# Earlier gates, copies and weight releases in the sublayer heads, a reordered mixer and moved buffers, in a two-layer trunk on one core

## The chip, the cores and the metric

The kernel runs on one core of one Trainium2 chip. The metric is the device time of one execution in microseconds, from a median of runs. The core's engines work beside each other, each through its own instructions in order: TensorE (PE, with its weight loads as PEld) multiplies matrices, VectorE (DVE) and ScalarE (ACT) work elementwise and move results out of the matmul banks, GpSimd (POOL) takes a few elementwise operations, and SyncE (SP) issues the DMA transfers.

## What is computed

The reference is a trunk of two layers on 512 tokens of width 1024 in float32. Each layer has a mixer and a feed-forward network (FFN), and each of the four sublayers is wrapped in the same way:

```python
def sandwich(x, mod, g_pre, g_post, fn):
    shift, scale, gate = mod
    h = rms_norm(x, g_pre) * (1.0 + scale[:, None]) + shift[:, None]
    return x + gate[:, None] * rms_norm(fn(h), g_post)

def swiglu(h, w_in, w_out):
    a, b = jnp.split(h @ w_in, 2, axis=-1)
    return (jax.nn.silu(a) * b) @ w_out

def modulation(c, w, b):
    return jnp.split(jax.nn.silu(c) @ w + b, 3, axis=-1)
```

The first layer's mixer joins two halves and projects them: means over windows of 2, 4, 8 and 16 tokens, each multiplied by a small matrix ("pooling"), and a gated linear recurrence with four heads (keys decay by a learned forget gate; the output is normed and multiplied by a silu gate). The second layer's mixer is a dilated attention with 24 heads in three groups and a relative bias. The FFN has 2816 hidden features.

## The kernel before

**Precision and tiling.** Each weight block of 128 x 1024 is loaded in float32 into the arena "f" and split into a high part (ScalarE, L353) and a low part (VectorE or GpSimd, through `sub`, L286). Each product then takes three matmuls: high by high, high by low and low by high. The activations `h_hi` and `h_lo` lie feature by token. All matmuls of this kind are recorded at L265, in the helper `mm`.

**Memory.** Three arenas hand out units of 512 columns: `ar` (zone "f" of 24 units, 8 of them for x), `rr` (the split weights: zones "r" of 14 and "o" of 4) and `tr` (zone "t" of 8). Two further zones, "s" (16 units) and "z" (12), belong now to `ar`, now to `rr`; `swing_to` hands them over. A free unit that was freed longest ago is taken first. Eight banks hold the matmul results. `load_next` issues a weight load when "f" has room, `split_next` splits a loaded block when `rr` has room, and `weights(i)` does both ahead by the counts in `ahead`. `fixed` (L313) limits some blocks to named zones. `weights_done(i)` gives a block's units back.

**What sets the order.** The program is written in one order, but a scheduler with a time model places the instructions; between `hold(...)` and `release()` the named engines keep the order of the text. In the first mixer only TensorE is held (L996); VectorE's and SP's order there is the scheduler's. `interleave` weaves the matmuls of one stage with a chain of norm steps of the sublayer before (`finish_half`), at places listed in `ENDS`.

**Modulation.** The modulation of each sublayer is computed on VectorE: 48 calls of `ada_step`, each of two halves (L405), where a half reduces a loaded 128 x 1025 tile against silu(c). The tiles come from a pool of three. Eight steps are done in the start, four beside the value blocks (`ADA[0]` is 12), four in the rest of the mixer (`ADA[1]` is 16) and four in `between`, up to 20.

**The start (L430 to L556).** TensorE broadcasts silu(c) with two matmuls, then does nine meaningless ones (`keep_warm`, `WARM`) until the squares of x are summed. The first projection runs over all eight banks.

**The first mixer (L892 to L1280).** Four value blocks (L1017), with levels of the recurrence's masked products between them (`level`, `grow`; the masks lie in "f", the accumulator too). Then the text for TensorE is: `mixed(0..3)` for the pooling input with more levels between them, and from L1208 `mixed(2)`, `pooled(0)`, `mixed(3)`, `blocks_64`, `pooled(1)`, `gate(0)`, `blocks_128`, `gate(1)`, `pooled(2)`, `keys_back(0)` and `(1)`, `gate(2)`, `pooled(3)`, `states(0)` and `(1)`, `gate(3)`, `outputs(0)` and `(1)`, `keys_back(2)` and `(3)`. `means(g)` (VectorE) computes the windowed means and splits them (`split_into`, L572 and L286); `pooled(g)` multiplies them. `states` writes the state S on VectorE (L1162, L1165), and `outputs` reads it. Then the output projection runs with `between(i)` after each of its first blocks.

**The heads (L863).** `project_head` begins an FFN or the attention: its first eight (FFN) or six (attention) weight blocks are multiplied first with one half of the tokens, in groups of three, while the norm of the other half is still being finished, and then with the other half. All its weights are released at the end. In the FFN, `gated` (L1293) then forms silu(a) b for the four pairs of blocks; in the attention, `keep_qk` (L1330) copies the six blocks' queries and keys out of the banks. Both free the banks. Behind the attention's head comes `values(0)`, which takes four banks, and `load_biases(0)` (L1356), which loads the first relative biases.

## Time and profile before

| what | value |
|---|---|
| median of 3 runs | 1267.06 us (1266.58 to 1270.38) |
| the profiled execution | 1271.72 us |
| its span, first to last instruction | 1269.9 us |
| mean granted TensorE clock | 0.988 |
| HBM read | 160.78 MB |
| weight and modulation loads | 512.0 and 512.5 KB each |

The page gives busy times per engine, a map of the span in 40 slices, the chain of work that ended last, and the costliest groups. In a row of a group, "x16" is the count, the two numbers behind the bar are the busy time in us and the mean of one in ns, and behind the second bar stands the idle time of the engine ahead of these instructions, with what ended it. In a timeline the columns are the start in us, the duration in us, the engine, the line, the operation, what it writes and reads, and in brackets the idle time just before it with what ended that. In a list of waits the numbers are the total in us, how many, and the longest. By stages, the span looks so (busy us):

| from, to (us) | stage | PE | DVE | ACT | clock |
|---|---|---|---|---|---|
| 0 to 17 | start | 12.82 | 9.15 | 9.99 | 1.00 |
| 17 to 57 | first projection | 39.50 | 37.44 | 16.89 | 1.00 |
| 275 to 570 | first FFN | 295.00 | 113.56 | 75.70 | 1.00 |
| 570 to 615 | end of it, attention head | 42.02 | 36.06 | 27.90 | 1.00 |
| 650 to 840 | attention | 189.08 | 78.24 | 68.40 | 1.00 |
| 840 to 920 | its end, second FFN's head | 72.83 | 58.55 | 50.85 | 0.98 |
| 945 to 1240 | second FFN | 295.00 | 79.56 | 72.09 | 1.00 |

### The profile page before, as it was taken

What the parts mean: (1) busy time and instruction counts of PE and PEld (TensorE: products, weight loads), DVE (VectorE), ACT (ScalarE), POOL (GpSimd) and SP (SyncE); (2) the same over time, 40 slices, a digit from 0 to 9 for tenths busy, and PEclk for the clock granted to TensorE, in tenths of its full rate; (3) what the DMA queues carried; (4) which work ended last, traced back from release to release, by engine and by line L of the source; (5) the groups of instructions that cost most, each with busy time, mean ns of one, the idle gap of its engine ahead of it and who ended that gap; (6) DMA issues with size and microseconds to landing.
All of it is one profiled execution on the core that took longest, in us unless ns stands there. A gap on an engine that the chain in (4) does not pass through costs nothing.

```text
span 1269.9 us, 20632 instructions
## 1 busy us (share of the span) xinstructions
PE 1231.6 (97%) x8672; PEld 1091.6 (86%) x8672; DVE 620.5 (49%) x974; ACT 461.7 (36%) x757; POOL 194.7 (15%) x110
## 2 busy tenths in 40 slices
PE   8999899999999999999999999999999999999997
PEld 6777699988888889998979878778998888889997
DVE  7978966754443223528485232455854222213415
ACT  4553445532222222326453233445732222222313
POOL 1000022321111111213211110022311111121002
PEclk9999899999999999999999999999999999999999
DMA  8943732336552133321378222123435222223302
GB/s 308 351 147 130 271 127 87 135 128 222 193 195 76 67 100 100 128 89 54 116 251 287 78 71 75 54 95 119 134 127 188 83 83 67 68 99 100 100 1 67
DMA packets 50383, 164.25 MB, mean 129 GB/s; under 512 B 5809, under 2 KB 11081, under 8 KB 50290
## 3 DMA queue, kind: packets, MB, share of 16 engines
q1 hardware_dynamic: 50290, 162.93, 37.8%
q8 instruction: 68, 1.11, 0.4%
q14 instruction: 25, 0.20, 0.0%
HBM read 160.78 MB, written 2.13 MB: 128 GB/s over the span
## 4 chain that ended last, share of the span: by engine, by line
PE 84%; DVE 7%; DMA 3%; ACT 2%; issue 2%; POOL 1%; SPq 0%; DVEq 0%; ACTq 0%; POOLq 0%
PE bank L265 81%; DMA ada_w<-ada 2%; DVE ada_w L405 1%; DVE r L286 1%; PE bank L1475 1%; DVE t L649 1%; PE bank L1444 1%; DVE f L653 1%; DMA f<-w_qf 1%; DVE h L688 0%; DVE t L610 0%; POOL h L286 0%; PE bank L936 0%; POOL cst L481 0%; DMA f<-w_ho 0%
## 5 line engine op out<-in xcount | busy, mean ns | idle before, releaser
L265 PE MATMUL bank<-h,r 128*128 128x512 f32 (+1 forms) x2096 | 457.5, 360 | 1.5 <-ACT h L529 0.7
L265 PEld LDWEIGHTS bank<-h,r 128*128 128x128 f32 x2096 | 358.9, 189 | 61.5 <-ACT h L529 2.0
L265 PE MATMUL bank<-h,swing 128*128 128x512 f32 (+1 forms) x1688 | 325.3, 341 | 1.2 <-DVE swing L1298 1.2
L265 PEld LDWEIGHTS bank<-h,swing 128*128 128x128 f32 x1688 | 269.9, 189 | 37.3 <-DVE swing L1298 1.4
L286 DVE TENSOR_TENSOR r<-f,r 128x1024 fp32r<-128x1024 f32 (+1 forms) x67 | 81.6, 1220 | 181.4 <-PE bank L265 98.5
L353 ACT ACTIVATE r<-f 128x1024 fp32r<-128x1024 f32 x105 | 110.3, 1058 | 140.3 <-PE bank L265 107.0
L265 PE MATMUL bank<-o,swing 128*128 128x256 f32 x1248 | 152.0, 275 | 0.0
L265 PEld LDWEIGHTS bank<-o,swing 128*128 128x128 f32 x1248 | 146.3, 188 | 0.1
L286 DVE TENSOR_TENSOR swing<-f,swing 128x1024 fp32r<-128x1024 f32 x49 | 66.3, 1357 | 133.4 <-PE bank L265 81.0
L405 DVE SCALAR_TENSOR_TENSOR ada_w<-ada_w,sil 128x1025 f32<-128x1025 f32 x96 | 126.2, 1328 | 10.3 <-DMA ada_w<-ada 9.2
L353 ACT ACTIVATE swing<-f 128x1024 fp32r<-128x1024 f32 x80 | 83.5, 1058 | 93.9 <-PE bank L265 51.5
L286 POOL TENSOR_TENSOR r<-f,r 128x1024 fp32r<-128x1024 f32 x24 | 58.7, 2445 | 323.6 <-PE bank L265 243.7
L265 PE MATMUL bank<-o,r 128*128 128x256 f32 x864 | 107.4, 276 | 0.0
L265 PEld LDWEIGHTS bank<-o,r 128*128 128x128 f32 x864 | 102.6, 188 | 0.2
L1297 ACT ACTIVATE t<-bank 128x512 f32<-128x512 f32 (+1 forms) x52 | 27.2, 531 | 176.2 <-PE bank L265 176.0
L286 POOL TENSOR_TENSOR swing<-f,swing 128x1024 fp32r<-128x1024 f32 x23 | 56.6, 2460 | 215.2 <-PE bank L265 175.5
L265 PE MATMUL bank<-h,o 128*128 128x512 f32 (+1 forms) x296 | 78.2, 350 | 1.7 <-DVE h L688 1.7
L265 PE MATMUL bank<-r,h 128*128 128x512 f32 x288 | 73.4, 404 | 0.6 <-ACT swing L907 0.6
L265 PEld LDWEIGHTS bank<-r,h 128*128 128x128 f32 x288 | 62.5, 252 | 8.1 <-ACT swing L913 1.2
L286 DVE TENSOR_TENSOR o<-f,o 128x256 fp32r<-128x256 f32 (+2 forms) x38 | 26.6, 717 | 73.7 <-ACT o L572 66.8
L265 PEld LDWEIGHTS bank<-h,o 128*128 128x128 f32 x296 | 52.6, 190 | 10.0 <-DVE h L688 2.1
L481 POOL TENSOR_TENSOR cst<-cst 128x2 f32<-128x2 f32 (+1 forms) x19 | 16.9, 891 | 275.8 <-DVE cst L479 275.8
(189 smaller groups left out, 1005.9 us busy)
## 6 DMA issues: line engine op xcount, KB each, us to landing
ada_w<-ada SPq DMA_DIRECT2D x96, 512.5 KB, 4.7
f<-w_fi SPq DMA_DIRECT2D x88, 512.0 KB, 4.5
f<-w_fo SPq DMA_DIRECT2D x44, 512.0 KB, 3.4
f<-w_aqk SPq DMA_DIRECT2D x24, 512.0 KB, 4.5
f<-w_av SPq DMA_DIRECT2D x12, 512.0 KB, 3.9
f<-w_qf SPq DMA_DIRECT2D x8, 512.0 KB, 7.2
f<-w_ho SPq DMA_DIRECT2D x8, 512.0 KB, 4.0
f<-x SPq DMA_DIRECT2D x8, 256.0 KB, 4.5
```

Of the source, the lines that this page charges most:

```text
L265: i = pe.matmul(o, lhsT, rhs, start=start, stop=stop, skip_group_check=True)
L286: eng.tensor_tensor(o, x, y, ALU.subtract)
L353: act.activation(hi, w, AF.Copy)
L405: return dve.scalar_tensor_tensor(w, w, 1.0, sil, ALU.mult, ALU.mult, accum_out=mods[:, s, 2 * j + k : 2 * j + k + 1])
L481: newest_rstd[0] = pool.tensor_tensor(r, v, mhalf[:, 0:cols], ALU.pow).ins.name
L649: dve.tensor_tensor(us[i], us[i], rows, ALU.mult)
L653: (pool if i < 2 else dve).tensor_tensor(x, x, us[i], ALU.add)
L1297: act.activation(tr.ap(sa)[:, cols], a, AF.Silu)
L1444: pe.matmul(o, qc, kc, start=True, stop=True, skip_group_check=True)
L1475: pe.transpose(bk[b][:, seg * P : (seg + 1) * P], sc[:, i * P : (i + 1) * P], ident)
```

## The change

**Start.** Four meaningless matmuls (`PREWARM`) stand ahead of the two that broadcast silu(c), and `WARM[0]` goes from 9 to 13.

**Mixer.** `ADA` goes from (12, 16) to (14, 15): two steps behind each of the first two value blocks and one behind the others, one in the rest of the mixer, and one more at `between(3)`. `pooled(1)` goes behind `gate(0)`, `pooled(2)` behind `gate(2)`, `pooled(3)` (with the release of its weights) behind `keys_back(3)`. Masks, accumulator and the four gates move to "t"; the transposed keys and the states S move from "t" to "z" and are freed at `between(2)`.

**Heads.** `project_head` releases a group's weights, and calls `done(banks, n)`, as soon as the group is through with the second half. In the FFN, `from_head` then gates the first two pairs (`N_EARLY`); their products lie in "f", and the twelve that lie in "z" are those after them, so "z" changes hands at block 14 of the down projection. In the attention, `from_head` copies queries and keys 0 and 1 behind the first group, into "f", and the other four at the end, into "s". The first biases get three units of "z", and the head's six weight blocks may lie only in "r", "s" and "o".

```diff
-WARM = 9, 5, 7
+PREWARM = 4
+WARM = 13, 5, 7
+N_EARLY = 2
-ADA = 12, 16
+ADA = 14, 15
...
-    fixed = [(w_av, w_ao - w_av, "ro"), (w_ao, 2, "h")]
+    fixed = [(w_qk, 6, "rso"), (w_av, w_ao - w_av, "ro"), (w_ao, 2, "h")]
...
-        fixed.append((w_fo[i], N_SWING2, "rs"))
+        fixed.append((w_fo[i], N_EARLY + N_SWING2, "rs"))
...
-    for i, b in enumerate(c_banks):
-        mm(b, bk[b], small[0:1, 0:1].broadcast_to([1, P]), c_row[:, i * T : (i + 1) * T], True, True)
     warm_r = ar.get(1)
     warm = ar.ap(warm_r, P)
     pool.memset(warm, 0.0)
+    for _ in range(PREWARM):
+        mm(c_banks[1], bk[c_banks[1]][:, 0:P], warm, warm, True, True)
+    for i, b in enumerate(c_banks):
+        mm(b, bk[b], small[0:1, 0:1].broadcast_to([1, P]), c_row[:, i * T : (i + 1) * T], True, True)
...
-    masks_r = ar.get(3)
+    masks_r = tr.get(3)
...
+                if hf:
+                    for i in group:
+                        weights_done(base + i)
+                    if group[-1] == n - 1:
+                        release()
+                    done(banks, group[-1] + 1)
...
-        for i in range(n):
-            weights_done(base + i)
-        release()
-        return banks
...
-    acc_r = [ar.get(1) for _ in range(1)]
+    acc_r = [tr.get(1) for _ in range(1)]
...
-        ada_step(ADA[0])
+        for _ in range(2 - kk // 2):
+            ada_step(ADA[0])
...
-        g_rs0.append(ar.get(1, "f"))
+        g_rs0.append(tr.get(1))
...
-            kst_rs.append(tr.get(1))
-            S_rs.append(tr.get(1))
+            kst_rs.append(ar.get(1, "z"))
+            S_rs.append(ar.get(1, "z"))
...
-    pooled(1)
     ahead.update(load=9, split=4, f=4)
     gate(0)
+    pooled(1)
...
-    pooled(2)
     keys_back(0)
     keys_back(1)
     ada_step(ADA[1])
     gate(2)
-    pooled(3)
-    rr.free(pwh_r)
-    rr.free(pwl_r)
+    pooled(2)
     states(0)
     states(1)
...
     keys_back(3)
+    pooled(3)
+    rr.free(pwh_r)
+    rr.free(pwl_r)
...
             outputs(3)
+            for r in (*kst_rs, *S_rs):
+                ar.free(r)
             swing_to(ar, rr)
...
         if i < 4:
             ada_step(20)
+        if i == 3:
+            ada_step(20)
...
+        def from_head(banks, n):
+            while len(g_rs) < min(n // 2, N_EARLY):
+                z = [x[len(g_rs)] for x in banks]
+                gated([bk[b][:, 0:HT] for b in z], [bk[b][:, HT:T] for b in z])
+                for b in z:
+                    bk.free(b)
+            if n == n_head:
+                head_banks.extend(banks)
...
+        def from_head(banks, n):
+
+            if n == N_QK:
+                rr.closed.discard("o")
+                swing_to(ar, ar)
+            for i in range(len(head_rs), N_QK if n == N_QK else 2):
+                r = ar.get(1, "f" if i < 2 else "s")
+                for hf in range(2):
+                    keep_qk(i, r, bk[banks[hf][i // 2]][:, (i % 2) * HT : (i % 2 + 1) * HT], hf)
+                head_rs.append(r)
+                if i % 2:
+                    for z in banks:
+                        bk.free(z[i // 2])
+
+        project_head(s, w_qk, N_QK, chain, from_head)
+        first_biases = ar.get(3, "z")
```

More of the change, by code (lines that the diff above doesn't have):

```diff
@@ L861, in out_project, with project_head @@
         return chain
-    def project_head(s, base, n, chain):
+    def project_head(s, base, n, chain, done):
         banks = []
@@ L1211, in trunk @@
     both(weights_32)
-    ar.free(acc_r[0])
-    ar.free(masks_r)
+    tr.free(acc_r[0])
+    tr.free(masks_r)
     mixed(3)
@@ L1287, in ffn @@
         g_rs = []
-        banks = project_head(s, base, n_head, chain)
-        rr.closed.add("o")
-        swing_to(rr, ar)
-        ahead.update(load=6, split=4, f=4, r=0)
         def gated(ab, bb):
-            sa, g = tr.get(1), ar.get(1, "z" if len(g_rs) < N_SWING2 else "f")
+            sa, g = tr.get(1), ar.get(1, "z" if N_EARLY <= len(g_rs) < N_EARLY + N_SWING2 else "f")
             for cols, a, b in zip(((0, T),) if len(ab) == 1 else ((0, HT), (HT, T)), ab, bb):
@@ L1300, in gated @@
             g_rs.append(g)
-        for f in range(NF):
+        def from_head(banks, n):
[6 more added lines that the diff above has]
+                head_banks.extend(banks)
+        head_banks = []
+        project_head(s, base, n_head, chain, from_head)
+        rr.closed.add("o")
+        swing_to(rr, ar)
+        ahead.update(load=6, split=4, f=4, r=0)
+        for f in range(N_EARLY, NF):
             if f < n_head // 2:
-                gated([bk[z[f]][:, 0:HT] for z in banks], [bk[z[f]][:, HT:T] for z in banks])
-                for z in banks:
-                    bk.free(z[f])
+                z = [x[f] for x in head_banks]
+                gated([bk[b][:, 0:HT] for b in z], [bk[b][:, HT:T] for b in z])
+                for b in z:
+                    bk.free(b)
                 continue
@@ L1325, in attention @@
         ahead.update(load=N_QK, split=N_QK - 1, f=8, r=0)
-        head_banks = project_head(s, w_qk, N_QK, chain)
-        rr.closed.discard("o")
-        swing_to(ar, ar)
+        head_rs = []
         def keep_qk(i, r, y, half=None):
@@ L1342, in keep_qk @@
                 dve.tensor_copy(o, y)
-        head_rs = []
-        for i in range(N_QK):
-            r = ar.get(1)
-            for hf in range(2):
-                keep_qk(i, r, bk[head_banks[hf][i // 2]][:, (i % 2) * HT : (i % 2 + 1) * HT], hf)
-            head_rs.append(r)
-        for z in head_banks:
-            for b in z:
-                bk.free(b)
+        def from_head(banks, n):
[12 more added lines that the diff above has]
+        first_biases = ar.get(3, "z")
         ahead.update(load=5, split=3, f=8, r=0)
@@ L1356, in load_biases @@
         def load_biases(pair):
-            r = ar.get(3)
+            r = ar.get(3) if pair else first_biases
             t = ar.ap(r, 2 * (W0 + 256)).rearrange("p (h n) -> p h n", h=2)
```

24 lines of the change are left out of this document (12 added, 12 removed).

## The prediction

> **What bounds the kernel now.** I read the page first (busy shares, chain), then the list of waits of TensorE, then stages by windows, then the timelines of the stages in which TensorE waits.
>
> ```profile
> PE 1231.6 (97%) x8672; PEld 1091.6 (86%) x8672; DVE 620.5 (49%) x974; ACT 461.7 (36%) x757; POOL 194.7 (15%) x110
> PE 84%; DVE 7%; DMA 3%; ACT 2%; issue 2%; POOL 1%; SPq 0%; DVEq 0%; ACTq 0%; POOLq 0%
> PE bank L265 <- ACT r L572: 5.0, 2, 4.3
> PE bank L265 <- DVE r L286: 2.5, 2, 1.5
> PE bank L265 <- DVE swing L1342: 2.0, 1, 2.0
> PE bank L265 <- DVE swing L1298: 1.4, 2, 1.2
> ```
>
> TensorE is the bound: 84% of the chain. The change removes no matmul that computes anything, so it can only win what TensorE waits or runs slow. The four waits quoted (5.0, 2.5, 2.0 and 1.4 us) are those that the moved steps touch: L572 and L286 are the split of the pooling means ahead of `pooled`, L1342 is a query/key copy after the attention head, L1298 a gate product after the FFN heads. By windows (busy us of PE, PEld, DVE, ACT, POOL, granted clock, DMA share, GB/s) the mixer's middle is another kind of stage than its neighbours:
>
> ```profile
> 57.30:114.00 56.70, 56.11 (x845) 43.47 (x846) 41.81 (x82) 25.45 (x37) 0.37 (x3) 0.97 0.45 161
> 114.00:163.10 49.10, 41.03 (x376) 33.34 (x376) 45.89 (x82) 24.58 (x41) 0.00 (x0) 0.86 0.70 250
> 163.10:230.00 66.90, 66.90 (x555) 66.17 (x554) 43.01 (x73) 35.86 (x89) 16.70 (x12) 1.00 0.24 82
> ```
>
> From 114 to 163 VectorE is busy 45.89 of 49.10 us and TensorE idles 8.07; before and behind it TensorE is full and VectorE has 14.9 and 23.9 us to spare. In this stretch VectorE is the bound.
>
> **The mixer's middle (L1214 to L1243).** The five waits of TensorE in it, where it reaches `outputs(0)`, and the last state copies on VectorE that `outputs(0)` needs:
>
> ```profile
> 122.16 0.70 PE L1114 MATMUL bank<-swing,swing 128*32 128x32 f32 x32 [0.53 <-DVE swing L948]
> 123.59 0.50 PE L265 MATMUL bank<-r,o 128*128 128x512 f32 x1 [0.74 <-ACT r L572]
> 125.19 1.22 PE L265 MATMUL bank<-r,o 128*128 128x512 f32 x2 [1.09 <-DVE r L286]
> 152.96 0.80 PE L265 MATMUL bank<-r,o 128*128 128x512 f32 x1 [4.26 <-ACT r L572]
> 155.22 1.22 PE L265 MATMUL bank<-r,o 128*128 128x512 f32 x2 [1.46 <-DVE r L286]
> 166.01 1.50 PE L265 MATMUL bank<-t,swing 128*128 128x128 f32 x12
> 162.10 0.98 DVE L1165 SCALAR_TENSOR_TENSOR t<-t,bank 128x128 f32<-128x128 f32 x3
> ```
>
> `pooled(1)` (123.59) and `pooled(3)` (152.96) stand in TensorE's fixed order before their split is there. The change puts `pooled(1)` behind `gate(0)`, `pooled(2)` behind `gate(2)` and `pooled(3)` behind `gate(3)`, `outputs(0)`, `outputs(1)` and two `keys_back`. The waits are 0.53 + 0.74 + 1.09 + 4.26 + 1.46 = 8.1 us. Behind both lies a stretch at half clock:
>
> ```profile
> 120.90:124.30 3.40, 1.93 (x66) 1.36 (x65) 3.40 (x8) 3.33 (x7) 0.00 (x0) 1.00 0.34 90
> 124.30:131.10 6.80, 5.92 (x14) 4.66 (x15) 6.80 (x11) 2.74 (x7) 0.00 (x0) 0.50 0.88 296
> 151.60:158.40 6.80, 3.98 (x14) 3.29 (x15) 6.33 (x11) 2.49 (x4) 0.00 (x0) 0.50 0.93 334
> 632.90:636.30 3.40, 1.37 (x7) 0.95 (x7) 3.40 (x7) 3.17 (x8) 0.00 (x0) 1.00 0.33 69
> 636.30:639.70 3.40, 3.40 (x10) 2.64 (x9) 3.40 (x7) 0.00 (x0) 0.00 (x0) 0.50 0.74 209
> ```
>
> Work done at clock 0.50 takes twice as long, so half of the busy time there, (5.92 + 3.98) / 2 = 5.0 us, is lost as well. For TensorE alone the stretch holds 8.1 + 5.0 = 13.1 us. But VectorE must follow. Its costliest work there is `ada_step`, which isn't due until the next sublayer:
>
> ```profile
> L405 DVE SCALAR_TENSOR_TENSOR ada_w<-ada_w,sil 128x1025 f32<-128x1025 f32 x16 | 19.6, 1226 | 2.3 <-DMA ada_w<-ada 2.3
> L405 DVE DVE_READ_ACCUMULATOR ada_w<-ada_w,sil 128x1 f32 x16 | 1.4, 86 | 0.0
> ```
>
> A half step costs 1.226 + 0.086 = 1.31 us, and 16 of them ran here: all eight steps of the text from L1224 to the last `between`, although four stand later in the text (only TensorE's order is fixed here, and the scheduler drew the others forward). The change takes steps 13 and 14 back to the value blocks: 4 half steps, 5.2 us. The step that it adds to `between(3)` replaces one of the four at L1224 to L1247, and I expect it to be drawn forward too, so 12 half steps stay. VectorE ended the state copies at 162.10 + 0.98 = 163.1; 5.2 us sooner is 157.9. TensorE came to `outputs(0)` at 166.0; unhindered it would come 13.1 sooner, at 152.9. The later of the two, 157.9, decides: **8.1 us** saved, between 0 (the copies stay late) and 13.1 (the scheduler puts them ahead of the half steps). Behind it TensorE is full and VectorE 64% busy (43.01 of 66.90), so the lead carries on. `pooled(3)` then has its split long ready.
>
> **The value blocks (L1028).** Here the 4 half steps, 5.2 us, arrive with four DMAs of `ada_w` on SP's queue.
>
> ```profile
> 86.35 1.23 DVE L286 TENSOR_TENSOR r<-f,r 128x1024 fp32r<-128x1024 f32 x1 [1.62 <-ACT r L353]
> 89.96 0.69 DVE L948 TENSOR_TENSOR swing<-swing,swing 128x512 f32<-128x512 f32 x1
> 92.30 1.32 PE L936 MATMUL bank<-swing,swing 128*32 128x32 f32 x128
> 93.10 0.45 DVE L937 COPY_PREDICATED f<-f,bank 128x256 f32<-128x256 int32 x1 [1.93 <-PE bank L936]
> 99.16 1.23 DVE L286 TENSOR_TENSOR r<-f,r 128x1024 fp32r<-128x1024 f32 x1 [2.62 <-issue]
> ada_w<-ada SPq DMA_DIRECT2D x96, 512.5 KB, 4.7
> ```
>
> VectorE's idle pieces there sum to 1.62 + 1.93 + 2.62 = 6.2 us, enough on the whole. But `grow` is queued behind the half steps, and TensorE's next level waits for it: it ended at 90.65, TensorE came at 92.30, so 1.65 us are free. One half step fits, two overrun by 1.0. I take half of that: **-0.5** (bounds 0 and, if each of the four also waits out its DMA's 4.7 us, 4 x 6.0 - 1.65 = 22).
>
> **The heads.** Rows of the copy and the gate that TensorE waits for:
>
> ```profile
> 634.66 2.07 DVE L1342 COPY swing<-bank 128x256 f32<-128x256 f32 x6
> 635.13 5.98 PE L265 MATMUL bank<-o,h 128*128 128x512 f32 x18 [2.03 <-DVE swing L1342]
> 272.20 2.07 DVE L1298 TENSOR_TENSOR swing<-t,bank 128x256 f32<-128x256 f32 x6
> 272.67 1.66 PE L265 MATMUL bank<-h,swing 128*128 128x512 f32 x6 [1.23 <-DVE swing L1298]
> 939.88 10.49 PE L265 MATMUL bank<-h,r 128*128 128x512 f32 x45 [0.16 <-DVE swing L1298]
> ```
>
> The attention head fills 6 of 8 banks and the first value block wants 4, so it waits 2.03 us until the copies free two. With the change queries and keys 0 and 1 are copied behind the first of two groups, one group (72 matmuls) before the end; the banks are then free in time. With the wait goes the half clock behind it, 3.40 / 2 = 1.7: **3.7 us**. On ScalarE and VectorE these copies now stand in the hand order, so the splits of the next blocks queue behind a wait for TensorE; but that group is finished when they are reached. The first biases get a place of their own in "z", and the transfer to it is not waited for today: 0. In the FFN heads two pairs are gated a group or two early, which frees four banks: 1.23 + 0.16 = **1.4 us**. Two gates then live in "f" throughout, and "z" turns over two blocks later; the "rs" zone still holds seven blocks ahead, so 0. Freeing the head's weights by group lets splits start sooner: 0, since nothing waits for one there. Bounds for the heads together: 0 to 5.1.
>
> Here a rule of the Trainium skill bears on the sum ("TensorE: Matmul & The Clock Gate", Part 1): the array falls to half clock after at least one idle window of about 3.4 us. The row 632.90 to 636.30 differs: 1.37 us busy of 3.40, so not wholly idle, and yet the next 3.40 us had 0.50. By the rule the 1.7 us would not hang on this wait and the sum would be 1.7 less; I follow the row.
>
> **The start.** `PREWARM` adds 4 matmuls (8 records) where TensorE sits idle until 3.26, and `WARM` 4 more (8 records) ahead of the row sums.
>
> ```profile
> 3.26 3.77 PE L265 MATMUL bank<-t,cst 1*128 1x512 f32 x4 [3.26 <-ACT t L454]
> 6.96 4.21 PE L265 MATMUL bank<-f 128*128 128x128 f32 x18
> 11.56 1.09 PE L265 MATMUL bank<-cst,t 128*128 128x1 f32 x8 [0.38 <-DVE t L497]
> 12.51 1.36 PE L265 MATMUL bank<-f 128*128 128x128 f32 x10
> ```
>
> The 18 records took 4.21 / 18 = 0.234 us each, those behind 12.51 0.136. Eight more at 0.234 make 1.9, less the 0.38 idle: at most 1.5 us later, and 0 if the earlier matmuls bring the full clock sooner. I take **-0.6**: the records turned fast between 11.2 and 11.6 here, so a part of the eight would run fast.
>
> **Regions.** Masks, accumulators and gates move to "t", states to "z". Their new places were last read long before by the order of freeing, and no TensorE wait names a region. "f" gains 8 units, room for 4 more blocks under way: 0 here, and a rival below.
>
> **Sum.** 8.1 + 3.7 + 1.4 - 0.5 - 0.6 = 12.1 us. Against the profiled execution: span 1269.9, 1271.72 with what lies around it; 1259.6. That execution lies 4.7 above the median of the runs, 1267.06; carried to it: **1255.0**. Own range: 1251 (half way to the mixer's 13.1, start and values at 0: 2.5 + 1.1 less) to 1259 (two half steps' worth of the mixer lost, 2.6, the start at 1.5, the values at 1.0).
>
> **Rivals.**
> 1. TensorE-bound mixer: the scheduler places the state copies ahead of the half steps, and the whole 13.1 comes back, 5.0 more: 1250. For it: two thirds of the half steps could wait. Against: it drew them forward before.
> 2. Ada data late: 8 free units let SP issue 4 more weight blocks (2 MB) ahead of `ada_w`; at the 334 GB/s of 151.60 to 158.40 that is 6.3 us, in which VectorE waits with the state copies behind. The mixer then gains 1.8: 1261. For it: VectorE waited 2.3 us for `ada_w` already, with the DMA share at 0.93. Against: 4 half steps' loads (2 MB) leave this stretch.
> 3. The heads change nothing, as the hand order delays copies and gates: 5.1 less, 1260.
> 4. Slower: in the value blocks each extra half step waits out its DMA ahead of `grow`. From the third such wait on (3 x 6.0 - 1.65 = 16.4, more than the gains of 12.6) the kernel is slower; with all four, 1267.06 - 12.6 + 22 = 1277. Against: the DMA share there is 0.45, and the buffers of `ada_w` turn over while VectorE has 6.2 us idle.
>
> 5. The half clock around 636 comes although the wait is gone, for some other cause: 1.7 us less, 1256.7. For it: the wait and the half clock come together only once in these rows of the heads. Against: it began as the row with 1.37 of 3.40 ended. It is what the rule of "TensorE: Matmul & The Clock Gate" above (the Trainium skill) leaves.
>
> **How the numbers follow.** Forecast 0.42, rival 1 0.17, rival 2 0.15, rival 3 0.10, rival 4 0.08, rival 5 0.08. 0.3% (3.8 us, about what a measurement of this kernel can tell) puts "faster" below 1263.3. All but rival 4 lie there, with 0.06 in their tails up to it: faster 0.85, same 0.08, slower 0.07. The range takes in the forecast and rivals 1, 2, 3 and 5 with the start's and the values' bounds: 1248 to 1263.
>
> **What would show it.** Right: no wait on L572 left in TensorE's list; `outputs(0)` near 158; 12 half steps instead of 16 in VectorE's list of this stretch, 4 more before it; no half clock around 636; no wait on L1342, nor on L1298. Wrong: a new wait of TensorE ahead of `outputs` or `states` above 5 us, waits on L947/L948 between 78 and 114, or VectorE idle for `ada_w` above the 2.3 us of now.

## The result and the profile after

| | median us (runs) | ratio to the kernel before, 95% interval |
|---|---|---|
| before | 1270.34 (18) | |
| changed | 1262.81 (18) | 0.9936, 0.9921 to 0.9950 |

The change saves 7.5 us of the medians, 8.1 by the ratio; both kernels measured again, beside the last experiments, give 11.1 by the ratio (0.9913). The intervals of the two overlap and reach from 6 to 14 us. The forecast was 12.1 saved, from the 1267.06 of the three runs then known to 1255.0; the result lies at the upper edge of its range (1248 to 1263). The profiled execution of the changed kernel took 1263.48 us, with a span of 1261.7 us and a clock of 0.993. From its page, the busy times and the chain that ended last; then the longest items of TensorE's list of waits (us in total, times, longest):

```profile
PE 1230.5 (98%) x8688; PEld 1092.7 (87%) x8688; DVE 623.4 (49%) x974; ACT 460.4 (36%) x757; POOL 195.4 (15%) x110
...
PE 85%; DVE 6%; issue 3%; DMA 2%; ACT 2%; POOL 2%; SPq 0%; DVEq 0%; ACTq 0%; POOLq 0%
```

```profile
PE bank L267 <- DVE t L623: 5.2, 5, 2.5
...
PE bank L267 <- ACT h L576: 1.4, 2, 0.9
PE bank L267 <- DVE h L288: 1.3, 1, 1.3
...
PE bank L267 <- DVE t L1196: 1.3, 1, 1.3
...
PE bank L267 <- DVE swing L288: 0.7, 1, 0.7
```

Lines have moved: L265 is now L267, L286 is L288, L353 is L355, L572 is L576, L405 is L407, L979 is L987. The four waits that the prediction named are gone: none on a pooling split (the L576 of now writes `h`), none on the copy or the gate product of a head. In their place are a row sum of 2.5 us (L623) and four waits of 0.7 to 1.3 us in the mixer's output projection. The mixer's three stages by windows, to be held against the windows of the prediction (clock in the column behind the engines):

```profile
57.50:118.20 60.70, 57.53 (x844) 44.07 (x843) 46.98 (x91) 25.55 (x37) 0.37 (x3) 0.94 0.56 198
118.20:155.80 37.60, 37.60 (x385) 31.58 (x385) 35.37 (x65) 20.99 (x37) 0.00 (x0) 1.00 0.61 216
155.80:196.90 41.10, 36.68 (x301) 35.57 (x299) 27.53 (x44) 20.53 (x58) 7.67 (x5) 1.00 0.45 152
```

The middle is now full for TensorE, 37.60 of 37.60 us. The stages on both sides of it have holes that they did not have. The last state copy on VectorE and `outputs(0)` on TensorE, to be held against 162.10 and 166.01 in the prediction:

```profile
152.15 0.34 DVE L1174 SCALAR_TENSOR_TENSOR swing<-swing,t,bank 128x128 f32<-128x128 f32 x1
155.82 1.50 PE L267 MATMUL bank<-swing,swing 128*128 128x128 f32 x12
```

One profile of each kernel is not enough to say by how much, so both were profiled once more, unaltered. Stage times, from the first matmuls of each in TensorE's timeline (us; around each sublayer's border stand four groups of row sums):

| stage | before, both profiles | changed, both profiles |
|---|---|---|
| start and first projection | 63.6, 66.1 | 63.9, 64.2 |
| first value block to last level | 51.5, 51.2 | 55.4, 53.3 |
| last level to the first gated head | 55.8, 54.2 | 44.0, 44.0 |
| from there to the mixer's first row sum | 30.1, 29.9 | 33.6, 35.1 |
| to the first row sum behind the first FFN | 371.3, 371.3 | 369.6, 369.5 |
| to the attention's first scores | 68.8, 67.2 | 67.5, 68.6 |
| to the last group of matmuls | 620.0, 618.5 | 618.9, 618.9 |
| sum | 1261.1, 1258.4 | 1252.9, 1253.6 |

So the middle gains 11.0 us on the mean of both, the FFN stages about 2, and the mixer's other two stages give 7.4 back; the attention head, forecast at 3.7, gives nothing.

"At full clock" below means: a stage's time less half of the time for which TensorE was busy in its stretches at clock 0.50. It is an estimate, and too low where TensorE would have waited anyway. In the expectations half of the whole stretches is taken off, TensorE's idle time included, so that some figures there are lower.

### The profile page after: what moved, and what is told of

It reads as the page before. It is cut to its first block, busy times and chain, and to the rows that moved or that the text cites. A ratio compares the mean times of both kernels' runs of the same rounds, so it can differ in the third digit from the quotient of the medians.

```text
span 1261.7 us, 20665 instructions
## 1 busy us (share of the span) xinstructions
PE 1230.5 (98%) x8688; PEld 1092.7 (87%) x8688; DVE 623.4 (49%) x974; ACT 460.4 (36%) x757; POOL 195.4 (15%) x110
## 4 chain that ended last, share of the span: by engine, by line
PE 85%; DVE 6%; issue 3%; DMA 2%; ACT 2%; POOL 2%; SPq 0%; DVEq 0%; ACTq 0%; POOLq 0%
PE bank L267 81%; DVE ada_w L407 1%; PE bank L1504 1%; DMA ada_w<-ada 1%; PE bank L1473 1%; DVE swing L288 1%; PE bank L944 1%; DMA swing<-hot 1%; DVE t L653 1%; DVE r L288 1%; DMA f<-w_qf 1%; POOL cst L485 0%; POOL swing L288 0%; POOL h L288 0%; ACT t L610 0%
## 5 line engine op out<-in xcount | busy, mean ns | idle before, releaser
L267 PE MATMUL bank<-h,r 128*128 128x512 f32 (+1 forms) x2088 | 454.4, 359 | 3.9 <-DVE h L692 1.7
L267 PEld LDWEIGHTS bank<-h,r 128*128 128x128 f32 x2088 | 356.4, 189 | 63.6 <-ACT h L576 2.1
L267 PE MATMUL bank<-h,swing 128*128 128x512 f32 (+1 forms) x1688 | 326.4, 342 | 2.9 <-DVE h L288 1.3
L267 PEld LDWEIGHTS bank<-h,swing 128*128 128x128 f32 x1688 | 270.7, 190 | 39.3 <-DVE h L288 1.5
L288 DVE TENSOR_TENSOR r<-f,r 128x1024 fp32r<-128x1024 f32 x67 | 81.5, 1219 | 170.9 <-PE bank L267 102.9
L355 ACT ACTIVATE r<-f 128x1024 fp32r<-128x1024 f32 x104 | 109.4, 1058 | 135.5 <-PE bank L267 96.1
L267 PE MATMUL bank<-o,swing 128*128 128x256 f32 x1248 | 151.8, 276 | 0.0
L267 PEld LDWEIGHTS bank<-o,swing 128*128 128x128 f32 x1248 | 146.3, 188 | 0.1
L288 DVE TENSOR_TENSOR swing<-f,swing 128x1024 fp32r<-128x1024 f32 x50 | 71.6, 1440 | 132.4 <-PE bank L267 75.0
L407 DVE SCALAR_TENSOR_TENSOR ada_w<-ada_w,sil 128x1025 f32<-128x1025 f32 x96 | 124.2, 1305 | 7.6 <-DMA ada_w<-ada 6.4
L355 ACT ACTIVATE swing<-f 128x1024 fp32r<-128x1024 f32 x80 | 82.8, 1060 | 77.4 <-PE bank L267 49.9
L288 POOL TENSOR_TENSOR r<-f,r 128x1024 fp32r<-128x1024 f32 x24 | 58.3, 2429 | 319.2 <-PE bank L267 248.7
L267 PE MATMUL bank<-o,r 128*128 128x256 f32 x864 | 107.3, 276 | 0.0
L267 PEld LDWEIGHTS bank<-o,r 128*128 128x128 f32 x864 | 102.5, 188 | 0.1
L288 POOL TENSOR_TENSOR swing<-f,swing 128x1024 fp32r<-128x1024 f32 x22 | 54.3, 2467 | 216.9 <-PE bank L267 174.5
L267 PE MATMUL bank<-h,o 128*128 128x512 f32 (+1 forms) x304 | 77.0, 349 | 0.0
L267 PE MATMUL bank<-r,h 128*128 128x512 f32 x288 | 74.2, 407 | 2.2 <-issue 1.1
L267 PEld LDWEIGHTS bank<-r,h 128*128 128x128 f32 x288 | 63.3, 255 | 9.8 <-ACT swing L915 1.5
L267 PEld LDWEIGHTS bank<-h,o 128*128 128x128 f32 x304 | 52.3, 188 | 7.9 <-ACT h L533 0.2
L485 POOL TENSOR_TENSOR cst<-cst 128x2 f32<-128x2 f32 (+1 forms) x19 | 17.2, 907 | 236.0 <-DVE cst L483 235.9
L576 ACT ACTIVATE o<-swing 128x512 fp32r<-128x512 f32 x24 | 15.3, 637 | 93.5 <-PE bank L267 93.5
```

Source lines behind the costliest of these rows:

```text
L267: i = pe.matmul(o, lhsT, rhs, start=start, stop=stop, skip_group_check=True)
L288: eng.tensor_tensor(o, x, y, ALU.subtract)
L355: act.activation(hi, w, AF.Copy)
L407: return dve.scalar_tensor_tensor(w, w, 1.0, sil, ALU.mult, ALU.mult, accum_out=mods[:, s, 2 * j + k : 2 * j + k + 1])
L485: newest_rstd[0] = pool.tensor_tensor(r, v, mhalf[:, 0:cols], ALU.pow).ins.name
L576: act.activation(hi, src, AF.Copy)
```

## The experiments

Each edit is made to the changed kernel, but for the second profile of the kernel before. Medians are of the runs shown; the ratio is to the kernel before, as measured beside it.

### Both kernels again

> The changed kernel unaltered, profiled once more. Theory (where half clock falls is decided by how the clock's 3.41 us windows happen to lie over the waits of one execution, not by the code): the stretches at half clock lie at other places than 66, 595 and 841 us, at least one of the three is gone or a new one is there, while every stage, with the half-clock loss taken out, agrees within 0.5 us with the first profile behind 122 us. Rival (half clock belongs to the code): the same three stretches, of 6.8, 3.4 and 3.4 us.

> The kernel before unaltered, profiled once more. Theory (as for the changed kernel): other stretches at half clock than 66, 124, 151, 636 and 848 us, though some at 120 to 160 us again, since TensorE's waits are longest there; from the last level to the mixer's first row sum about 79 us with the half-clock loss taken out, as before. Rival: the same five stretches.

Changed: 1261.10 us (6 runs), 0.9913, 0.9892 to 0.9935. Before, the profiled execution alone: 1268.99 us. Half clock, changed kernel: from 66.4 (6.8 us), 595.4 and 841.2 (3.4 each) the first time; from 67.0 (3.4), 186.5 (3.4), 592.6 (6.8) and 841.8 (3.4) the second: behind the same three waits again, at other lengths, and behind one more. Kernel before: the five stretches from 66 to 848 the first time; between the first projection and the last matmul only one the second time, from 153.0 (6.8 us). At full clock the stages of the changed kernel behind 122 us agree within 0.3 us. In the kernel before, the stretch from the last level to the gated head differs by 0.8 (50.8 and 51.6); the others agree within 0.2. Counted as in the expectation it differs by 1.8 (49.0 and 50.8), because TensorE was busy for only 4.03 of the 6.83 us at half clock from 151.6; from the last level to the row sum that gives 80.7 us the second time, not the 79 expected. The theory holds in part. The times at full clock agree, but the same three places came again, as the rival has it: half clock goes with the waits, and which wait gets it, and for how long, changes from one execution to the next. The wait in the changed kernel's row sum, then the same wait in the kernel with the states in "f" (below), then the same place in the attention in the changed kernel and in the one with the poolings back, each followed by its next window:

```profile
592.02:595.43 3.41, 1.67 (x12) 1.49 (x13) 2.27 (x5) 3.41 (x5) 1.02 (x2) 1.00 0.00 0
595.43:598.84 3.41, 3.41 (x18) 3.41 (x18) 3.41 (x2) 0.06 (x1) 2.61 (x1) 0.50 0.00 0
837.78:841.19 3.41, 1.71 (x14) 1.50 (x13) 3.11 (x7) 1.35 (x5) 2.10 (x1) 1.00 0.54 172
841.19:844.60 3.41, 3.41 (x18) 3.41 (x18) 2.66 (x6) 2.15 (x5) 2.38 (x1) 0.50 0.38 141
```

```profile
587.30:590.71 3.41, 1.58 (x14) 1.38 (x12) 3.17 (x7) 2.98 (x8) 0.06 (x1) 1.00 0.15 29
590.71:594.13 3.42, 2.49 (x19) 2.32 (x20) 2.38 (x5) 2.65 (x3) 1.85 (x2) 1.00 0.00 0
```

```profile
834.30:837.71 3.41, 1.71 (x14) 1.53 (x13) 3.30 (x7) 1.39 (x4) 1.83 (x1) 1.00 0.65 186
837.71:841.13 3.42, 3.42 (x48) 2.89 (x46) 2.68 (x6) 1.83 (x5) 2.38 (x1) 1.00 0.32 126
```

Behind 1.67 and 1.71 us of TensorE work in a window came half clock; behind 1.58 and 1.71 in others it did not. And in the second profile of the kernel before, the wait for L1342 that the prediction charged with 1.7 us of half clock has none behind it; it lay so that its window still held 2.08 us of work:

```profile
634.30:637.71 3.41, 2.08 (x9) 1.71 (x10) 3.41 (x8) 2.27 (x6) 0.00 (x0) 1.00 0.45 128
637.71:641.13 3.42, 3.42 (x39) 2.42 (x37) 2.96 (x6) 1.09 (x2) 1.24 (x1) 1.00 0.75 256
```

All stretches inside the work are whole multiples of 3.41 us long. The Trainium skill ("TensorE: Matmul & The Clock Gate", Part 1) says that the window runs freely, 3413 ns long, and does not start with the kernel; the traces agree. Its rule that half clock needs an idle window doesn't hold here, at 1.67 us busy of 3.41.

### The mixer's steps, poolings and states, one at a time

```diff
-ADA = 14, 15
+ADA = 12, 16
...
-        for _ in range(2 - kk // 2):
-            ada_step(ADA[0])
+        ada_step(ADA[0])
...
-        if i == 3:
-            ada_step(20)
```

> Only the places of the ada steps go back: one in each value block, four ahead of outputs(0), none in between(3). Theory (the half steps sit in VectorE's fixed order and delay what is behind them): the value blocks get back most of what they lost, so the last level's matmuls end near 116 instead of 119.3; ahead of the first four state copies VectorE now holds 6 half steps and 3 half-width splits more, about 9 us, of which 3.3 were free, so outputs(0) comes near 160 instead of 155.8; the total is 1 to 4 us above the changed kernel. Rival (the value blocks lost their time to the later biases' transfers, and the middle won its time by the order of the poolings alone): the last level stays at 119 and outputs(0) at 156, the total within 1 us of the changed kernel.

Measured: 1267.71 us (10 runs), 0.9968, 0.9946 to 0.9989. From the last level to the gated head 49.1 us instead of 44.0 (46.7 at full clock), with two new waits:

```profile
PE bank L267 <- DVE swing L1173: 2.2, 1, 2.2
PE bank L267 <- ACT r L576: 2.0, 1, 2.0
```

So the middle went as the theory has it. In all the kernel lost 4.9 us of the medians, 4.1 by the ratios. The value blocks did not: the last level came at 116.8, but the stretch from the first to the last level took 38.9 us at full clock, not less than with the new steps (37.0 to 38.2 in ten profiles). What the value blocks lost is not due to the half steps.

For the second, the three `pooled` calls go back to their places in the text.

```diff
+    pooled(1)
     ahead.update(load=9, split=4, f=4)
     gate(0)
-    pooled(1)
...
+    pooled(2)
     keys_back(0)
...
     gate(2)
-    pooled(2)
+    pooled(3)
+    rr.free(pwh_r)
+    rr.free(pwl_r)
...
     keys_back(3)
-    pooled(3)
-    rr.free(pwh_r)
-    rr.free(pwl_r)
```

> Only the poolings go back: pooled(1) ahead of gate(0), pooled(2) ahead of the first keys_back, pooled(3) ahead of the states. Theory (the middle won because VectorE had less ahead of the state copies): ahead of these copies stand one half step, one split and one half-width split more, 3.2 us, which the 3.3 us of slack nearly hold, but TensorE waits at the poolings again, 1 to 4 us with what half clock follows; outputs(0) near 158 to 160. Rival (the order of the poolings is what won the 11.8 us of the middle): outputs(0) at 166, total at the kernel before.

Measured: 1261.51 us (5 runs), 0.9920, 0.9892 to 0.9949. Neither side: no pooling wait came back, the middle took 42.9 us instead of 44.0, and the out projection 34.4 instead of 33.6. The order of the poolings, the change's most visible edit, shows no worth in this one profile, once VectorE has less ahead of it.

```diff
-            kst_rs.append(ar.get(1, "z"))
-            S_rs.append(ar.get(1, "z"))
+            kst_rs.append(ar.get(1, "f"))
+            S_rs.append(ar.get(1, "f"))
```

> Only the place of kst and S: region f instead of z. Theory (states in z keep the three splits into z out of the middle, to pile up in the out projection): three splits come ahead again, VectorE holds two half steps, one split and three half-width splits more ahead of the first state copies, 5.9 us, of which 3.3 were free, so gated_head(0) moves from 163.3 to about 166; the out projection, from there to its first row sum, shrinks from 33.6 to about 30.0 us; the total is within 1 us of the changed kernel, or up to 2 below. Rival (the out projection is longer because TensorE reaches it 7.6 us sooner and VectorE cannot follow): it stays at 33 to 34 us and the total rises by 2 to 3.

Measured: 1262.08 us (7 runs), 0.9933, 0.9911 to 0.9955. The out projection shrank to 29.9 us at full clock, as before the change; the middle grew to 46.4 at full clock, with a half-clock stretch on top. Between 120 and 205 us the waits of TensorE are these two alone, where the changed kernel has five between 120 and 200:

```profile
PE bank L267 <- DVE t L1196: 3.2, 1, 3.2
PE bank L267 <- DVE f L1174: 0.6, 1, 0.6
```

VectorE's timelines show why. With the states in "f", two of the three splits into "z" are done by 155 us; in the changed kernel "z" holds the states until `between(2)`, and these splits stand, with the next ones, between the steps that TensorE waits for:

```profile
147.97 1.22 DVE L288 TENSOR_TENSOR swing<-f,swing 128x1024 fp32r<-128x1024 f32 x1
...
153.72 1.22 DVE L288 TENSOR_TENSOR swing<-f,swing 128x1024 fp32r<-128x1024 f32 x1
```

```profile
177.05 1.23 DVE L288 TENSOR_TENSOR swing<-f,swing 128x1024 fp32r<-128x1024 f32 x1
...
178.79 5.67 DVE L288 TENSOR_TENSOR swing<-f,swing 128x1024 fp32r<-128x1024 f32 x3
184.39 0.74 DVE L1207 SCALAR_TENSOR_TENSOR f<-bank,cst,t 128x512 f32<-128x512 f32 x1
```

From the last level to the row sum, both stages together are 76.3 us at full clock here, 77.6 and 77.4 in the two profiles of the changed kernel, 80.8 and 81.5 in those of the kernel before. So the place in "z" costs 1.2 us on balance, too little for the medians to show.

### The place of the masks

```diff
-    masks_r = tr.get(3)
+    masks_r = ar.get(3)
...
-    acc_r = [tr.get(1) for _ in range(1)]
+    acc_r = [ar.get(1) for _ in range(1)]
...
```

> Only the masks and the accumulator go back from t to f. In all profiles with the masks in t TensorE waits 1 to 2 us for a split just behind the second level (at 91.1 us in the changed kernel, 87 to 89 in three others); in the kernel before there is no such wait, and it is there with the old ada steps too. Theory (the place of the masks changes what f takes in, and so the order of the splits): the wait goes, the stretch from the first to the last level takes 36.7 instead of 37 to 38.9 us, 1 to 2 us less in all. Rival (that wait hangs on nothing but the order in which the scheduler put TensorE's instructions, or on late transfers): it stays at 1 to 2 us and the total within 1 us.

Measured: 1261.24 us (4 runs), 0.9911, 0.9875 to 0.9946. The rival: the wait behind the second level is still there (0.8 us, at 87.7), and first to last level took 37.7 us. That it is a wait for a split, as the expectation says, is not shown. In the changed kernel the split beside it ended at 90.45, 0.65 us before TensorE went on, and the profile names nothing that TensorE waited for ("issue"); in the kernel with the copies in "s" (below) TensorE went on at 87.85, 0.26 us before that split ended.

```profile
89.22 1.23 DVE L288 TENSOR_TENSOR r<-f,r 128x1024 fp32r<-128x1024 f32 x1 [0.63 <-ACT r L355]
91.10 4.06 PE L267 MATMUL bank<-r,h 128*128 128x512 f32 x17 [1.10 <-issue]
```

### The heads alone

All of the start and the mixer go back to the kernel before; only the heads' edits stay.

> Only the edits behind the mixer stay (pairs and copies behind their groups, the zones, the place of the first biases); start, mixer and ada steps are those of the kernel before. Theory (the heads hold about half of the change): the first FFN, from the last row sum of the mixer to its own first, takes 328.8 instead of 330.5 us; from the second head's last row sum to the first scores 27.3 instead of 30.4; the second FFN 335.2 instead of 335.7; together 4 to 6 us below the kernel before. Rival (the mixer holds nearly all of it and the heads only follow): at most 2 us below.

Measured: 1267.25 us (10 runs), 0.9961, 0.9938 to 0.9985, about 5.0 us below the kernel before by the ratio. The stages came as the theory has them (first FFN 328.8, 27.3 to the first scores, second FFN 335.2). But in the head the third row sum has the wait that the changed kernel has, and the stage from the FFN's row sum to the first scores took 67.6 us, against 68.8 and 67.2. No half clock lies in it here, as in the 67.2: from the fourth row sum to the first scores it is 1.5 us shorter, from the second to the fourth 1.9 longer (29.0 against 27.1). The FFN stages account for 2.2 us; for the rest of the 5.0, whose interval runs from 1.9 to 7.9, the profile shows no place.

```diff
-N_EARLY = 2
+N_EARLY = 0
```

> Only the two pairs of each FFN head are gated behind the whole head again, with the zones that go with it. Theory: the waits for the gate products come back, the first FFN takes about 330 us instead of 328.8 and the second 335.6 instead of 335.2: 1.2 to 2 us in all. Rival (the first FFN won its 1.7 us by freeing the head's weights by group, or the waits are filled by other work): both FFN stay within 0.3 us of the changed kernel.

Measured: 1265.08 us (10 runs), 0.9936, 0.9918 to 0.9954. First FFN 330.6, second 335.6; the wait for the gate product is back (behind the mixer, then behind the attention):

```profile
PE bank L267 <- DVE swing L1307: 1.3, 1, 1.3
```

```profile
PE bank L267 <- DVE swing L1307: 0.2, 1, 0.2
```

The theory holds by the stages: 1.8 + 0.4 = 2.2 us, of which the two waits are 1.5. The runs alone don't settle it: the ratio is the changed kernel's first one (0.9936), but the two kernels below and above that were measured beside it (copies late, masks in "f") are 2.7 and 3.8 us faster.

For the attention head, first the copies alone went back behind the head, then the places too:

```diff
-            for i in range(len(head_rs), N_QK if n == N_QK else 2):
+            for i in range(N_QK if n == N_QK else 0):
```

> Only the copies of queries and keys 0 and 1 go back behind the whole attention head; zones and freeing by group stay. Theory: TensorE waits about 2 us for these copies again ahead of the first value block, so that from the head's last row sum to the first scores it takes 28.7 us at full clock instead of 27.3, and 1.7 more if half clock follows: 1.4 to 3.1 us in all. Rival (the freeing of the head's weights by group, with the place of the first biases, made this gain): the stretch stays at 27.3.

```diff
-            for i in range(len(head_rs), N_QK if n == N_QK else 2):
-                r = ar.get(1, "f" if i < 2 else "s")
+            for i in range(N_QK if n == N_QK else 0):
+                r = ar.get(1)
...
-        first_biases = ar.get(3, "z")
...
-            r = ar.get(3) if pair else first_biases
+            r = ar.get(3)
```

> Copies of queries and keys 0 and 1 behind the whole head and into region s, and the first biases wherever there is room, as in the kernel before; the zone of the head's weights and the freeing by group stay. With the copies late but in f there was no wait. Theory (the wait of the kernel before hung on the place: s is still read as the head's last weights, so copies into it wait for the head's last matmul): a wait of about 2 us at the first value block is back, 28.7 us at full clock from the last row sum to the first scores instead of 27.3. Rival (the freeing of the weights by group removed it): 27.3 stays.

Copies late: 1262.38 us (5 runs), 0.9912, 0.9878 to 0.9946, and 27.3 us to the first scores, no wait for a copy. The theory fell. Late and in "s": 1262.82 us (4 runs), 0.9933, 0.9914 to 0.9953, 29.1 us to the first scores, and

```profile
PE bank L267 <- DVE swing L1364: 1.2, 2, 0.7
```

So it is the place that removed the wait for L1342, not the earlier copying. That the two went back with the biases' place leaves open which of the two places counts; the row names the copy.

### The split that moved to GpSimd

In the changed kernel the second attention value block is split on GpSimd into "o" while VectorE writes the head's `h` (VectorE, GpSimd, TensorE):

```profile
584.35 5.42 DVE L692 SCALAR_TENSOR_TENSOR h<-t,cst,h 128x256 fp32r<-128x256 f32 x4
```

```profile
583.63 2.50 POOL L288 TENSOR_TENSOR r<-f,r 128x1024 fp32r<-128x1024 f32 x1 [4.33 <-ACT r L355]
586.84 2.66 POOL L288 TENSOR_TENSOR o<-f,o 128x1024 fp32r<-128x1024 f32 x1 [0.71 <-ACT t L610]
```

```profile
593.56 0.58 PE L267 MATMUL bank<-cst,t 128*128 128x1 f32 x4 [2.54 <-DVE t L623]
```

Of 48 such writes (ns: shortest, median, longest) the median takes 476 ns; the two here that began after a GpSimd split had begun took 2.06 and 2.65 us.

```profile
L692 DVE SCALAR_TENSOR_TENSOR h<-t,cst,h x48: 471/476/2646, 211.3 to 912.0; 128x256 fp32r<-128x256 f32 x48
```
The edit gives that one split to VectorE and changes no other instruction's place.

```diff
-        sub(lo, w, hi.bitcast(F32), share[0], by)
+        sub(lo, w, hi.bitcast(F32), share[0], dve if i == w_av + 1 else by)
```

> One instruction changes its engine: the split of the second attention value block (1024 wide, into o) runs on VectorE instead of GpSimd, behind the four writes to h. Theory (GpSimd's split stretched two writes to h on VectorE, 475 ns each elsewhere, to 2.06 and 2.65 us, and this made the row sum late): these two take about 0.5 us, 3.7 us less, against 1.2 us for the split; the wait of 2.54 us ahead of the row sum at 593.6 falls below 0.7, the half clock from 595.4 to 598.8 goes; 2 to 4 us less in all. Rival (the stretch comes from the other GpSimd split, or from ScalarE, or these writes are not what the row sum waits for): the wait stays at 1.5 to 3.7 us and the total within 1 us.

Measured: 1261.13 us (10 runs), 0.9923, 0.9903 to 0.9943. The rows that answer (VectorE, TensorE):

```profile
582.55 3.25 DVE L692 SCALAR_TENSOR_TENSOR h<-t,cst,h 128x256 fp32r<-128x256 f32 x4
585.72 1.21 DVE L288 TENSOR_TENSOR o<-f,o 128x1024 fp32r<-128x1024 f32 x1
```

```profile
590.71 0.58 PE L267 MATMUL bank<-cst,t 128*128 128x1 f32 x4 [1.54 <-ACT r L355]
...
593.23 0.73 PE L267 MATMUL bank<-cst 128*128 128x128 f32 x4 [1.13 <-POOL cst L485]
```

The mechanism is shown: the four writes fell from 5.42 to 3.25 us. It is only half of the wait, though: the write beside the other GpSimd split stays long, the row sum still waits 1.54, and GpSimd's small step L485, now beside a VectorE split, makes the next wait 1.13 instead of 0.21. With this edit VectorE's rows are those of the kernel before, where TensorE waited only 0.71 us, because three matmuls of the first value block (0.87 us) stood ahead of the row sum (VectorE, TensorE):

```profile
590.10 3.25 DVE L688 SCALAR_TENSOR_TENSOR h<-t,cst,h 128x256 fp32r<-128x256 f32 x4
593.28 1.21 DVE L286 TENSOR_TENSOR o<-f,o 128x1024 fp32r<-128x1024 f32 x1
```

```profile
596.60 0.87 PE L265 MATMUL bank<-o,h 128*128 128x512 f32 x3
598.18 0.60 PE L265 MATMUL bank<-cst,t 128*128 128x1 f32 x4 [0.71 <-DVE t L619]
```

The changed kernel does these three later, with the rest of the block. So of the 1.83 us by which the wait grew, 1.00 is the split on GpSimd; the other 0.83 is work that moved. Why the scheduler no longer puts it there was not tried. From the second of the border's row sums to the third the edit wins its 1.0 us back (14.8 us, against 15.8 in the changed kernel and 14.7 before). From the third to the fourth it loses 0.7 of it (13.9, against 13.2 and 12.5), with one window at half clock there, as in the changed kernel. The 13.2 is also what the kernels with the states in "f" and with the heads alone take with no half clock in it: TensorE then waits 1.7 to 1.8 us there instead of 0.2. So in the changed kernel one window at half clock costs nothing there, since TensorE would only wait longer; nearly two, in its second profile, make it 14.3.

### Two edits together

```diff
-            kst_rs.append(ar.get(1, "z"))
-            S_rs.append(ar.get(1, "z"))
+            kst_rs.append(ar.get(1, "f"))
+            S_rs.append(ar.get(1, "f"))
...
-        sub(lo, w, hi.bitcast(F32), share[0], by)
+        sub(lo, w, hi.bitcast(F32), share[0], dve if i == w_av + 1 else by)
```

> Both single edits that came out below the changed kernel: the states in f, and the split of the second value block on VectorE. Theory (they act in different stages, the mixer's out projection and the attention head): at full clock about 2 us below the changed kernel, of which the first gives 1.5 to 2 and the second 0 to 0.7; measured median 1259 to 1261. Rival (the earlier state splits only shift waits, and what the out projection wins, half clock ahead of it takes): the median of the changed kernel within 1 us.

Measured: 1260.73 us (6 runs), 0.9912, 0.9897 to 0.9928, against 1261.10 for the changed kernel beside it. Within what was measured this is no faster. At full clock the profile shows the out projection at 30.1 us and the middle at 46.2, much as with the states alone.

## Why the prediction was right, and where it was wrong

**The mixer's middle (8.1): the bound was right, the size was 11.0, and it did not carry on.** VectorE was the bound. The forecast left it the bound, with `outputs(0)` waiting for the state writes. What came is rival 1's case: the writes ended at 152.5, 3.3 us ahead of `outputs(0)` at 155.8, and TensorE was full up to there. (155.8 against the forecast 157.9 understates this, as the last level ended 4.2 us later than in the forecast's profile.) The step that failed in the size is that 12 half steps "stay" ahead of the state writes: they stayed in the stage, but between the last level's masked copy and the last of the four writes, VectorE's timeline held 14 half steps and 7 weight splits before, and 6 and 4 after. The scheduler put four half steps behind the writes, and two of the three splits are those that "z" was taken for. Of the 11.0, 7.2 are won at full clock. Putting the half steps back costs 5.1 us there, 2.7 of them at full clock, and putting the states into "f" costs 2.4; no single edit shows the rest.

**Regions (0): wrong.** The states in "z" are what took those two splits out, and the out projection paid 3.6 us for them at full clock (33.6 against 30.0), shown by moving the states alone, which costs 2.4 of it again in the middle. The prediction asked when a place was last read, not what its new owner keeps from starting. The sentence "the lead carries on" is the step that failed: VectorE had time to spare there, but its list was in the wrong order.

**The value blocks (-0.5): the sign right, the cause wrong.** The stage lost 3.0 us on the mean of the two profiles. Of that, 1.7 is half clock; at full clock, from the first to the last level, 38.1 and 38.2 us stand against 36.7 and 36.7. No wait on L955 or L956 appeared, and neither the old steps nor the masks' old place mends it. What there is instead is the wait behind the second level, which no kernel with the old start and mixer has. It changes from one execution to the next: in nine profiles in which the four engines' instructions are in the same order up to the last level (the changed kernel's two, and those of the edits to poolings, states, heads and the one split) it is between none and 1.3 us, and the stretch between 37.0 and 38.2, 37.7 on the mean. So 1.0 us of the loss is shown, and the two profiles overstate it. Its cause is open. In the ten profiles that have this wait, TensorE goes on 2.3 to 2.6 us after a packet of 16384 bytes starts on the queue that loads instructions (88.53 and 91.10 in the changed kernel). So it may be waiting for its own instructions, of which the new start puts more ahead. The old start with the changed mixer, which would tell, was not tried, nor the gates' place.

**The attention head (3.7): nothing.** The wait of 2.03 us went, but for the place of the copies, not their time, and it is worth 1.5. Its half clock (1.7) was a matter of that one execution. And between the second and the fourth row sum the head lost 1.9 again: 1.1 up to the third, of which a split on GpSimd is 1.0, and 0.7 from there to the fourth, for which no run shows the cause. The step that failed is "Freeing the head's weights by group lets splits start sooner: 0, since nothing waits for one there": a split that starts sooner can stand in the way of another engine. That the freeing by group is what made it sooner was not tried alone.

**The FFN heads (1.4): right, at 2.2.** 330.6 in both profiles became 328.8, and 335.6 became 335.2; gating the pairs late again gives it all back.

**The start (-0.6): right within the spread.** The first projection began at 17.2 and 20.3 before, at 17.4 and 17.6 after. The 20.3 is an execution in which full clock came at 19.9 us instead of 11.7; in the eleven profiles with the new start it came between 10.1 and 12.6, so the early matmuls may save 3 us in some executions. Three profiles with the old start, one of them late, don't settle that.

**The half clock as a fixed price: wrong for the head, and too firm for the mixer.** The prediction took 5.0 us of the mixer's 13.1 and 1.7 of the head's 3.7 from where one execution had its half clock. The head's did not come again; the middle's was 2.6 in the second profile and 5.9 in the kernel with the heads alone, whose mixer is the old one. By the mean granted clock, the 11 runs of the kernel before that were measured beside 6 of the changed one lack 0.97% of 1270.3 us and 0.58% of 1259.6: 12.4 and 7.3 us. (23 and 18 runs that were not measured beside each other give 11.9 and 8.3.) So at most 4 to 5 us of the gain are clock, less where TensorE waited at half clock. By the profiles TensorE idles 29.7 and 31.3 us before and 22.7 and 22.0 after; of these 8.2 us fewer, 2.7 are idle time of the start, now filled with meaningless matmuls, and 5.5 are waits.

**The sum (12.1): in the range partly by luck.** On the mean of the two profiles, the middle won 2.9 us more than forecast, the FFNs 0.8 and the start 1.4; against that stand misses of 4.4 in the out projection, 2.5 in the value blocks and 3.7 in the head. That these offset each other in part no step of the prediction foresaw.

## What to carry to other kernels

Before pricing a moved buffer at nothing, ask what its new place would have taken in meanwhile, and where that work will stand instead. An engine with time to spare in a stage still makes others wait if its work arrives in one heap; read its order there, not its share. Half clock behind a short wait is a chance, not a price: take a second profile of the same kernel before charging a stage with it. And where the engine would wait for another anyway, half clock can cost nothing.

## What the runs showed of the hardware

Half clock does not follow from a wait alone. In fourteen profiles, behind the first 12 us, every window of 3.41 us with 0.43 or less of it busy on TensorE was followed by one at 0.50; between 0.45 and 0.61 some were and some were not. Above that, among windows that were themselves at full clock, it followed only around 63 us, beside the first biases' narrow matmuls, on windows that were 0.77 to 0.83 busy. Equal programs differ with it: the 18 runs of the kernel before took 1266.58 to 1277.29 us, and of 20 measured later the fastest (1266.39) had a mean granted clock of 0.993 and the slowest (1277.71) 0.983.

A VectorE write of 128x256 with two inputs in SBUF that began while GpSimd ran a 128x1024 subtraction lasted until 0.28 us after its end: 2.65 us instead of 0.48. So did all 66 such writes to `h` in the fourteen profiles, within 0.01 us; operations with one of their two inputs in a matmul bank kept their time (0.68 to 0.69 us for 123 of 128x512). The Trainium skill ("SBUF — State Buffer", section "Who interferes with whom") says that the later of two such operations waits for the whole of the first; the rows above agree.
